# Feed-forward of the sample: first products by Strassen's scheme, their squares through DRAM, second products as a stage of their own

## The chip, the cores and the metric

One core of one Trainium2 chip runs the whole program. The metric is the device time in microseconds of one execution; for the kernel before it is 2505.32 us, the median of three runs (2496.89 to 2509.4). The engines are TensorE (PE in the rows, its weight loads PEld), VectorE (DVE), ScalarE (ACT), GpSimd (POOL) and SyncE (SP, which here only issues DMAs). POOL issues DMAs too, on a queue of its own.

## The reference, cut to what matters

One encoder layer is applied to two sequences: a prompt of 512 tokens and a sample of 1024, both 1024 wide, with the same weights. The change concerns the second half of the layer, for the sample:

```
u = _layer_norm(x) * (1.0 + sc2) + sh2
h = jnp.dot(jnp.square(jax.nn.relu(jnp.dot(u, w_ff1))), w_ff2)
x = _layer_norm_affine(ALPHA * x + (1.0 + g2) * h, ln_ff_g, ln_ff_b)
```

`w_ff1` is 1024 x 4096 and `w_ff2` 4096 x 1024, all in float32.

## The kernel before

Everything lies in tiles of 128 partitions. Tokens are worked on in chunks of 512: the prompt is one chunk, the sample two. A float32 operand is split into a rounded part and a remainder (`hi`, `lo`; `fp32r` in the rows), and a product of two such pairs is three matmuls into one PSUM bank (`mm3`, lines 112 to 114). ACT makes the rounded part and DVE the remainder; `wunit` (lines 88 to 94) does so for a weight block of 128 x 1024 that SP loads into one of three shared buffers (`wraw`), with a multiplication by a gain on POOL (line 90) where one is given.

The feed-forward is `ff`. It goes in eight groups of four blocks of 128 hidden channels. For each block, `wstat` multiplies the block's w1 with the 8 k-tiles of u, for every chunk: 24 matmuls of 512 columns a chunk. ACT takes the positive part (line 859), DVE squares (860), and the square is split into hh and hl (863, 864). When four blocks are there, the second products follow: per chunk 4 token tiles and 2 halves of the output, each 12 matmuls, added into the running output y by DVE (885). The last group treats the chunks one after the other, so w1 is read a third time for its four blocks; there x1 is added (845 to 847) and w2 carries the gain, and each finished token tile is normed (`ln_stats`, lines 128 to 143) and stored (`ff_store`, 913 to 922). The prompt's feed-forward comes first, woven with the norm of the sample's second chunk; then `ff_load` (lines 821 to 825) loads and splits the sample's u from DRAM, and the sample's feed-forward runs over two chunks at once.

The order on each engine is set by a planner, which takes the instructions as the program emits them and moves one forward where, by its own cost estimates, its inputs and its buffer are ready; each engine then keeps that order. `weave` sets the emission: it steps the generator with the least progress. Pools are stacks on the left and right side of SBUF; a pool opened over a closed one waits tile by tile for the old tiles' last use.

## Time and profile before

| | |
|---|---|
| median of three runs | 2505.32 us |
| profiled execution, own time | 2501.49 us |
| its span (first to last instruction) | 2499.7 us |
| PE busy | 2380.8 us (95%), 10992 matmuls |
| DVE busy | 1479.1 us (59%) |
| ACT busy | 973.2 us (39%) |
| POOL busy | 483.6 us (19%) |
| mean granted TensorE clock | 0.980 of full speed |
| chain that ended last | PE 68%, DVE 10%, issue 8%, DMA 6% |

The profile is one execution. A busy PE means that matmuls are in flight; they overlap, so the spacing of their starts says how fast they go, not their own length. An idle time stands with the instruction before which it lay and with what ended it.

### The profile page before, as it was taken

To read this page: it belongs to the slowest core of one execution; us is meant where nothing else is said; L and a number is where in the kernel's file an instruction comes from. 1 tells how busy PE (TensorE), PEld (TensorE's weight loads), DVE (VectorE), ACT (ScalarE), POOL (GpSimd) and SP (SyncE) were. 2 spreads that over 40 slices of the span, in tenths; PEclk is the share of its full clock that TensorE was granted. 3 is DMA by queue.
4 is the path that set the end of the run, shared out by engine and by line. 5 is a ranking of instruction groups with operands and counts; after the bars stand their busy time and mean duration, and the time that the engine had idled before them with its cause. 6 is when DMAs were issued, how large, how long until landed. Compare 5 with 4: busy or idle time off the path is not lost.

```text
span 2499.7 us, 29827 instructions
## 1 busy us (share of the span) xinstructions
PE 2380.8 (95%) x10992; PEld 1896.8 (76%) x10992; DVE 1479.1 (59%) x2511; ACT 973.2 (39%) x1589; POOL 483.6 (19%) x524
## 2 busy tenths in 40 slices
PE   5989999988999999999999999998999999999997
PEld 3867777756777777777777788886888888888876
DVE  6998686464677754675967844445733333333466
ACT  4434656434677754553434233232411211221122
POOL 4341242443000014432322000003100000000133
PEclk9999999988999999999999999999999999999999
DMA  6767634576212127655656435233511210211231
GB/s 250 253 220 229 213 129 158 145 208 206 64 55 74 51 73 203 175 190 189 212 194 230 147 101 160 69 118 122 163 42 34 68 51 20 66 57 36 68 110 60
DMA packets 124227, 325.85 MB, mean 130 GB/s; under 512 B 20240, under 2 KB 35632, under 8 KB 124080
## 3 DMA queue, kind: packets, MB, share of 16 engines
q1 hardware_dynamic: 105744, 266.21, 34.8%
q0 software_dynamic: 18048, 57.69, 6.6%
q8 instruction: 87, 1.43, 0.2%
q14 instruction: 60, 0.49, 0.1%
q10 hardware_dynamic: 288, 0.03, 0.0%
HBM read 261.99 MB, written 62.93 MB: 130 GB/s over the span
## 4 chain that ended last, share of the span: by engine, by line
PE 68%; DVE 10%; issue 8%; DMA 6%; POOL 3%; ACT 2%; SPq 0%; POOLq 0%; DVEq 0%; ACTq 0%
PE D L112 18%; PE D L114 18%; PE D L113 18%; PE S L534 3%; PE T L552 3%; PE A L680 2%; DVE wlo L94 2%; PE A L565 2%; PE A L566 1%; PE T L673 1%; ACT whi L93 1%; PE S L657 1%; DMA wraw<-in_wada 1%; DVE junk L248 1%; DMA og<-g 1%
## 5 line engine op out<-in xcount | busy, mean ns | idle before, releaser
L93 ACT ACTIVATE whi<-wraw 128x1024 fp32r<-128x1024 f32 x266 | 279.3, 1057 | 839.2 <-PE D L114 408.1
L114 PE MATMUL D<-uh,wlo 128*128 128x512 f32 x1344 | 533.5, 397 | 8.5 <-DVE wlo L94 8.5
L112 PE MATMUL D<-uh,whi 128*128 128x512 f32 x1344 | 536.1, 399 | 3.3 <-DVE stk L341 1.3
L113 PE MATMUL D<-ul,whi 128*128 128x512 f32 x1344 | 532.6, 396 | 0.0
L94 DVE TENSOR_TENSOR wlo<-wraw,whi 128x1024 fp32r<-128x1024 f32 x250 | 315.9, 1265 | 300.7 <-ACT whi L93 299.6
L112 PE MATMUL D<-whi,hh 128*128 128x512 f32 x768 | 304.8, 398 | 8.0 <-ACT hh L863 7.8
L114 PEld LDWEIGHTS D<-uh,wlo 128*128 128x128 f32 x1344 | 255.3, 190 | 66.2 <-DVE wlo L94 10.8
L114 PE MATMUL D<-whi,hl 128*128 128x512 f32 x768 | 303.8, 398 | 0.8 <-DVE hl L864 0.6
L113 PE MATMUL D<-wlo,hh 128*128 128x512 f32 x768 | 303.3, 397 | 0.0
L112 PEld LDWEIGHTS D<-uh,whi 128*128 128x128 f32 x1344 | 255.3, 190 | 58.6 <-issue 2.4
L113 PEld LDWEIGHTS D<-ul,whi 128*128 128x128 f32 x1344 | 255.6, 190 | 53.7 <-issue 0.9
L885 DVE TENSOR_TENSOR y<-y,D 128x512 f32<-128x512 f32 x168 | 115.2, 686 | 214.6 <-PE D L114 214.1
L112 PEld LDWEIGHTS D<-whi,hh 128*128 128x128 f32 x768 | 145.5, 190 | 45.2 <-ACT hh L863 11.9
L846 POOL TENSOR_TENSOR y<-y,g 128x1024 f32<-128x1024 f32 x12 | 28.8, 2401 | 753.7 <-DVE y L885 753.7
L114 PEld LDWEIGHTS D<-whi,hl 128*128 128x128 f32 x768 | 145.3, 190 | 37.2 <-DVE hl L864 3.6
L113 PEld LDWEIGHTS D<-wlo,hh 128*128 128x128 f32 x768 | 145.7, 190 | 33.4
L537 DVE TENSOR_REDUCE m<-S 128x1 f32<-128x1024 f32 (+1 forms) x96 | 99.7, 1041 | 44.5 <-PE S L534 44.3
L112 PE MATMUL D<-whi,uh 128*128 128x512 f32 (+1 forms) x288 | 107.1, 374 | 13.6 <-DVE stk L341 7.7
L556 DVE TENSOR_TENSOR pl<-T,ph 128x512 fp32r<-128x512 f32 x160 | 107.0, 684 | 14.6 <-ACT ph L555 13.7
L555 ACT ACTIVATE ph<-T 128x512 fp32r<-128x512 f32 x160 | 93.4, 596 | 52.1 <-PE T L552 50.4
L113 PE MATMUL D<-wlo,uh 128*128 128x512 f32 (+1 forms) x288 | 105.7, 367 | 3.1 <-DVE wlo L94 3.1
L114 PE MATMUL D<-whi,ul 128*128 128x512 f32 (+1 forms) x288 | 105.3, 366 | 0.0
(172 smaller groups left out, 3862.1 us busy)
## 6 DMA issues: line engine op xcount, KB each, us to landing
wraw<-in_w SPq DMA_DIRECT2D x132, 512.0 KB
wraw<-in_wst SPq DMA_DIRECT2D x56, 512.0 KB
wraw<-in_wada SPq DMA_DIRECT2D x32, 512.0 KB
g<-gst POOLq DMA_DIRECT2D x48, 256.0 KB, 3.2
og<-g SPq DMA_DIRECT2D x48, 256.0 KB
wraw<-in_wab SPq DMA_DIRECT2D x24, 512.0 KB
wraw<-in_wo SPq DMA_DIRECT2D x24, 512.0 KB
raw<-in_wada_k SPq DMA_DIRECT2D x16, 512.0 KB
```

The costliest lines, as they stand in the source:

```text
L93: nc.scalar.activation(hi, raw, AF.Copy)
L94: (engine or nc.vector).tensor_tensor(lo, raw, hi, op=ALU.subtract)
L112: mm(out, l[0], r[0], start=start, stop=False)
L113: mm(out, l[0], r[1], start=False, stop=False)
L114: mm(out, l[1], r[0], start=False, stop=stop)
L534: nc.tensor.matmul(S[:, k * CH:(k + 1) * CH], q, K[r][:, k * CH:(k + 1) * CH], start=r == 0, stop=r == 1)
L537: nc.vector.tensor_reduce(m, S[:, :T], axis=AX.X, op=ALU.max, negate=True)
L552: nc.tensor.transpose(tp[:, qt * P:(qt + 1) * P], Ps[qt][:, k * P:(k + 1) * P], self.ident)
L555: nc.scalar.activation(ph, tp, AF.Copy)
L556: nc.vector.tensor_tensor(pl, tp, ph, op=ALU.subtract)
L565: nc.tensor.matmul(acc, V[:, k, :], ph, start=k == 0, stop=False)
L885: nc.vector.tensor_tensor(y[:, hs], y[:, hs], ps, op=ALU.add)
```

## The change

Two blocks of hidden channels (a pair) and the two chunks of the sample make a 2 x 2 scheme, with the inner dimension of 1024 halved too. In place of the eight block products of 512 x 512 (per pair 8 x 4 x 3 matmuls), seven are computed from sums of weight halves and of u halves, and DVE sums them up out of PSUM (`ff1_pairs`). The sums of u are made on POOL while the prompt's feed-forward runs (`sums_first`); two of them, and u itself, go through DRAM and are loaded again (`sums_next`, `sums_last`). The sums of weights are made on POOL one pair ahead (`pair_weights`), whose w1 come by POOL's queue. The squares go to DRAM and not into SBUF. When all 16 pairs are done, `ff2_groups` runs the second products as a stage of their own, in the same eight groups of four blocks, each group's w2 and squares loaded one group ahead into two alternating places; the gain and x1 are added behind group 6, and the last group covers both chunks in one go. The prompt keeps `ff`, with fewer buffers, with its outputs stored by POOL's queue, and with its last tile's tail on POOL as for the other tiles.

```diff
-                        hh = pool.tile([P, CH], F32R, tag="hh", name="hh", bufs=8)
-                        hl = pool.tile([P, CH], F32R, tag="hl", name="hl", bufs=8)
+                        hh = pool.tile([P, CH], F32R, tag="hh", name="hh", bufs=6)
+                        hl = pool.tile([P, CH], F32R, tag="hl", name="hl", bufs=6)
...
-                    Y = [[ypool.tile([P, D], F32, tag="y", name="y", bufs=8) for _ in range(TT)] for _ in chs]
+                    Y = [[ypool.tile([P, D], F32, tag="y", name="y", bufs=4) for _ in range(TT)] for _ in chs]
...
-                    self.ff_store(cst(), *late, tail=cs[-1] == len(chs) - 1)
+                    self.ff_store(cst(), *late)
...
+    def split(self, pool, raw, tag, bufs, engine=None):
+        hi = pool.tile([P, CH], F32R, tag="uh" + tag, name="uh", bufs=bufs)
+        lo = pool.tile([P, CH], F32R, tag="ul" + tag, name="ul", bufs=bufs)
+        if engine:
+            engine.tensor_copy(hi, raw)
+        else:
+            self.nc.scalar.activation(hi, raw, AF.Copy)
+        (engine or self.nc.vector).tensor_tensor(lo, raw, hi, op=ALU.subtract)
+        return hi, lo
+
+    def fetch(self, pool, src, tag, bufs, engine=None):
...
+        self.nc.sync.dma_start(lo.bitcast(F32), src)
+        self.nc.scalar.activation(hi, lo.bitcast(F32), AF.Copy)
+        (engine or self.nc.vector).tensor_tensor(lo, lo.bitcast(F32), hi, op=ALU.subtract)
+        return hi, lo
...
+    def sums_first(self, pool, raws, B):
...
+        for i in range(4):
+            r1, r2 = [raws.tile([P, D], F32, tag="raw", name="raw", bufs=2) for _ in range(2)]
+            nc.gpsimd.dma_start(r1, s["u2"][i][:, :])
+            nc.gpsimd.dma_start(r2, s["u2"][4 + i][:, :])
+            yield (i + 0.5) / 4
+            B["11"].append(self.split(pool, r1[:, ab], "s", 12, nc.gpsimd))
+            B["21"].append(self.split(pool, r2[:, ab], "s", 12, nc.gpsimd))
+            sub = lambda o, x, y: nc.gpsimd.tensor_tensor(o, x, y, op=ALU.subtract)
+            sub(r1[:, ab], r1[:, b], r1[:, ab])
+            nc.gpsimd.dma_start(s["t1"][i], r1[:, ab])
+            sub(r1[:, b], r2[:, b], r1[:, b])
+            nc.gpsimd.dma_start(s["t3"][i], r1[:, b])
+            sub(r2[:, b], r2[:, b], r1[:, ab])
+            B["t2"].append(self.split(pool, r2[:, b], "s", 12, nc.gpsimd))
+            sub(r2[:, ab], r2[:, ab], r2[:, b])
+            nc.gpsimd.dma_start(s["t4"][i], r2[:, ab])
+            yield (i + 1.0) / 4
+
+    def sums_next(self, pool, B):
+        for k in ("t1", "t3"):
+            for i in range(4):
+                B[k].append(self.fetch(pool, self.scr[1][k][i], "p", 8))
+
+    def sums_last(self, pool, B):
+        s = self.scr[1]
+        for i in range(4):
+            B["t4"].append(self.fetch(pool, s["t4"][i], "v", 8))
+        for i in range(4):
+            B["22"].append(self.fetch(pool, s["u2"][4 + i][:, CH:], "v", 8))
+
+    def pair_weights(self, p, fw, A, raws=None):
...
+            if early:
+                hi = fw.tile([P, D], F32R, tag="whi1", name="whi", bufs=2)
+                lo = fw.tile([P, D], F32R, tag="wlo1", name="wlo", bufs=2)
+            else:
+                hi = self.W.tile([P, D], F32R, tag="whi", name="whi", bufs=4)
+                lo = self.W.tile([P, D], F32R, tag="wlo", name="wlo", bufs=4)
+            nc.scalar.activation(hi, raw, AF.Copy)
+            nc.vector.tensor_tensor(lo, raw, hi, op=ALU.subtract)
+            return (hi[:, ab], lo[:, ab]), (hi[:, b], lo[:, b])
...
+        if p:
+            r1, r2 = [self.wraw(a["w1"][2 * p + j], queue=nc.gpsimd) for j in range(2)]
...
+        A["11"], A["12"] = halves(r1, not p)
+        yield
+        S = fw.tile([P, D], F32R, tag="wlo1", name="ws", bufs=2).bitcast(F32)
+        nc.gpsimd.tensor_tensor(S[:, ab], r2[:, ab], r2[:, b], op=ALU.add)
+        nc.gpsimd.tensor_tensor(S[:, b], S[:, ab], r1[:, ab], op=ALU.subtract)
+        A["s1"], A["s2"] = halves(S)
+        yield
+        w = fw.tile([P, D], F32R, tag="whi1", name="w22", bufs=2)
+        nc.scalar.activation(w[:, ab], r2[:, b], AF.Copy)
+        nc.vector.tensor_tensor(w[:, b], r2[:, b], w[:, ab], op=ALU.subtract)
+        A["22"] = (w[:, ab], w[:, b])
+        yield
+        nc.gpsimd.tensor_tensor(r2[:, ab], r1[:, ab], r2[:, ab], op=ALU.subtract)
+        nc.gpsimd.tensor_tensor(r2[:, b], r1[:, b], S[:, b], op=ALU.subtract)
+        A["s3"], A["s4"] = halves(r2)
+
+    def ff1_pairs(self, A, B, fw, pool):
...
+        def prod(l, r):
+            ps = self.dps()
+            for k in range(4):
+                ks = slice(k * P, (k + 1) * P)
+                self.mm3(ps, (l[0][:, ks], l[1][:, ks]), r[k], k == 0, k == 3)
+            return ps
+
+        def store(h, f, c):
+            nc.sync.dma_start(s["h"][f][:, c * CH:(c + 1) * CH], h)
+
+        def hidden(x, ps, f, c):
+            h = pool.tile([P, CH], F32, tag="h", name="h", bufs=5)
+            nc.vector.tensor_tensor(h, x, ps, op=ALU.add)
+            nc.vector.scalar_tensor_tensor(h, h, 0.0, h, op0=ALU.max, op1=ALU.mult)
+            store(h, f, c)
+
+        def part(x, ps):
+            u = pool.tile([P, CH], F32, tag="part", name="part", bufs=4)
+            nc.vector.tensor_tensor(u, x, ps, op=ALU.add)
+            return u
+
+        for p in range(16):
+            f, nxt = 2 * p, {}
+            ahead = self.pair_weights(p + 1, fw, nxt) if p < 15 else iter(())
+            ps = prod(A["11"], B["11"])
+            p1 = pool.tile([P, CH], F32, tag="part", name="part", bufs=4)
+            nc.scalar.activation(p1, ps, AF.Copy)
+            next(ahead, None)
+            hidden(p1, prod(A["12"], B["21"]), f, 0)
+            next(ahead, None)
+            u2 = part(p1, prod(A["s2"], B["t2"]))
+            ps = prod(A["s1"], B["t1"])
+            u4 = part(u2, ps)
+            next(ahead, None)
+            u3 = part(u2, prod(A["s3"], B["t3"]))
+            hidden(u3, ps, f + 1, 1)
+            next(ahead, None)
+            hidden(u3, prod(A["22"], B["t4"]), f + 1, 0)
+            hidden(u4, prod(A["s4"], B["22"]), f, 1)
...
+    def ff2_groups(self, places, ypool, cst):
...
+        def load(gi):
+            hpool, tag, homes = places[gi % 2]
+            W2, H = [], []
+            for f in range(G):
+                n = gi * G + f
+                W2.append(self.wunit(a["w2"][n], gain=g2 if gi == ng - 1 else None, **homes[f]))
+                raw = self.wraw(s["h"][n][:, :])
+                H.append([self.split(hpool, raw[:, c * CH:(c + 1) * CH], tag, 8) for c in range(2)])
+            return W2, H
+
+        nxt = load(0)
+        for gi in range(ng):
+            last = gi == ng - 1
+            (W2, H), late = nxt, None
+            if not last:
+                nxt = load(gi + 1)
+            for c in range(2):
+                for t in range(TT):
+                    y = Y[c][t]
+                    for hf in range(2):
+                        hs = slice(hf * CH, (hf + 1) * CH)
+                        ps = self.dps()
+                        for f in range(G):
+                            hh, hl = H[f][c]
+                            self.mm3(ps, (hh[:, t * P:(t + 1) * P], hl[:, t * P:(t + 1) * P]),
+                                     (W2[f][0][:, hs], W2[f][1][:, hs]), f == 0, f == G - 1)
+                        if gi == 0:
+                            nc.vector.tensor_copy(y[:, hs], ps)
+                        else:
+                            nc.vector.tensor_tensor(y[:, hs], y[:, hs], ps, op=ALU.add)
+                    if gi == ng - 2:
+                        t0 = c * CH
+                        x1 = self.wraw(s["x1"][t0 + t * P:t0 + (t + 1) * P, :])
+                        nc.gpsimd.tensor_tensor(y, y, g2, op=ALU.mult)
+                        nc.vector.scalar_tensor_tensor(y, x1, ALPHA, y, op0=ALU.mult, op1=ALU.add)
+                    if last:
+                        now = ((1, c * CH), t, y, *self.ln_stats(cst, [y], "f"))
+                        if late:
+                            self.ff_store(cst, *late)
+                        late = now
+            if last:
+                self.ff_store(cst, *late, tail=True)
...
-            nc.sync.dma_start(self.y[seq][t0 + t * P:t0 + (t + 1) * P, hs], y[:, hs])
+            (nc.sync if seq else nc.gpsimd).dma_start(self.y[seq][t0 + t * P:t0 + (t + 1) * P, hs], y[:, hs])
...
+                **{f"t{n}": [t(f"t{n}{i}_", [P, CH]) for i in range(4)] for n in (1, 3, 4)}, h=[t(f"h{i}_", [P, T]) for i in range(32)] if q else []))
...
-        w1 = [a["w1"][f] for f in range(32)]
-        ws = self.stream(w1 + w1 + w1[-4:], pool=wp, tag="1", bufs=2, ahead=1)
+        ws = self.stream([a["w1"][f] for f in range(32)], pool=wp, tag="1", bufs=2, ahead=1)
...
+            for x in self.sums_first(late["u"], late["raw"], B):
+                yield LN + 0.5 * x
...
-        US = [self.ff_load(scs[0], late["u"], "s"), self.ff_load(scs[1], upF, "p")]
-        self.weave(self.ff(scs, US, ws, hp, yp, consts))
-        for x in (y_st, h_st, late["ust"], late["st"], w_st, uF_st, psD_st):
+        A = {}
+        for _ in self.pair_weights(0, wp, A, late["raw"]):
+            pass
+        self.sums_next(upF, B)
+        late["rst"].close()
+        y_st.close()
+        h_st.close()
+        fv, fv_st = self.pool("fv", side="right")
+        fa, fa_st = self.pool("fa", side="right")
+        self.sums_last(fv, B)
+        self.weave(self.ff1_pairs(A, B, wp, fa))
+        late["ust"].close()
+        fa_st.close()
+        fv_st.close()
+        fh2, fh2_st = self.pool("fh2")
+        yp, y_st = self.pool("fy2", side="right")
+        own, fw, wts = dict(pool=fh2, tag="2", bufs=2), dict(pool=wp, tag="1", bufs=2), {}
+        self.ff2_groups([(fh2, "t", [own, own, fw, fw]), (upF, "p", [wts] * 4)], yp, late["pool"])
...
```

## Rows read from the trace of the kernel before

**Rows 1.** The page: engines (busy, share, instructions), and GB/s in 40 slices.

```profile
PE 2380.8 (95%) x10992; PEld 1896.8 (76%) x10992; DVE 1479.1 (59%) x2511; ACT 973.2 (39%) x1589; POOL 483.6 (19%) x524
...
GB/s 250 253 220 229 213 129 158 145 208 206 64 55 74 51 73 203 175 190 189 212 194 230 147 101 160 69 118 122 163 42 34 68 51 20 66 57 36 68 110 60
```

**Rows 2.** Busy time by stretches: length, each engine (x instructions), clock, DMA, GB/s.

```profile
core 0: us, PE busy (x) PEld busy (x) DVE busy (x) ACT busy (x) POOL busy (x), PEclk, DMA share, GB/s
...
1650.00:1700.00 50.00, 50.00 (x218) 40.63 (x217) 21.62 (x27) 11.67 (x15) 2.39 (x1) 1.00 0.24 75
1700.00:1767.00 67.00, 58.75 (x241) 46.67 (x241) 45.75 (x70) 24.44 (x35) 21.88 (x12) 0.95 0.49 149
1767.00:2406.00 639.00, 639.00 (x2762) 519.20 (x2761) 246.78 (x318) 132.15 (x182) 33.68 (x17) 1.00 0.20 61
2406.00:2471.00 65.00, 60.33 (x242) 46.81 (x241) 42.54 (x77) 19.53 (x27) 16.21 (x13) 0.95 0.22 73
```

**Rows 3.** Groups by form, 1767 to 2488 us: busy, mean ns, idle before, releaser.

```profile
L114 PE MATMUL D<-uh,wlo 128*128 128x512 f32 x512 | 202.2, 395 | 3.4 <-DVE wlo L94 3.4
L112 PE MATMUL D<-whi,hh 128*128 128x512 f32 x512 | 202.2, 395 | 0.3 <-ACT hh L863 0.3
...
L94 DVE TENSOR_TENSOR wlo<-wraw,whi 128x1024 fp32r<-128x1024 f32 x67 | 85.6, 1279 | 130.9 <-ACT whi L93 130.8
...
L93 ACT ACTIVATE whi<-wraw 128x1024 fp32r<-128x1024 f32 x67 | 70.1, 1058 | 404.2 <-PE D L114 235.1 <-DMA wraw<-in_w 100.1 <-PE D L113 52.7
L864 DVE TENSOR_TENSOR hl<-h,hh 128x512 fp32r<-128x512 f32 x64 | 44.2, 691 | 37.1 <-ACT hh L863 37.1
...
L921 POOL TENSOR_TENSOR y<-y,lnfb 128x512 f32<-128x512 f32 x16 | 23.3, 1463 | 22.2 <-DVE y L920 20.8 <-DVE rs_t L133 1.4
...
L847 DVE SCALAR_TENSOR_TENSOR y<-wraw,y 128x1024 f32<-128x1024 f32 x8 | 12.0, 1497 | 20.3 <-POOL y L846 20.3
```

**Rows 4.** Timeline of PE, 2406 to 2413 us: start, length, instruction.

```profile
2406.26 0.40 PE L113 MATMUL D<-ul,whi 128*128 128x512 f32 x1
2408.80 0.67 PE L114 MATMUL D<-uh,wlo 128*128 128x512 f32 x1 [2.15 <-DVE wlo L94]
...
2412.55 0.40 PE L114 MATMUL D<-uh,wlo 128*128 128x512 f32 x1
```

**Rows 5.** Timeline, DVE beside POOL, at 1715 and at 2429 us.

```profile
1715.05 2.39 POOL L90 TENSOR_TENSOR wraw<-wraw,g 128x1024 f32<-128x1024 f32 x1
1715.13 3.40 DVE L847 SCALAR_TENSOR_TENSOR y<-wraw,y 128x1024 f32<-128x1024 f32 x1 [2.52 <-POOL y L846]
...
2429.48 0.68 DVE L885 TENSOR_TENSOR y<-y,D 128x512 f32<-128x512 f32 x1
2429.64 1.29 POOL L921 TENSOR_TENSOR y<-y,lnfb 128x512 f32<-128x512 f32 x1 [3.61 <-DVE y L920]
...
2430.08 1.41 DVE L920 TENSOR_TENSOR y<-y,lnfg 128x512 f32<-128x512 f32 x1
```

**Rows 6.** Timeline at the prompt's end, 1718 to 1784 us: SP, PE and DVE.

```profile
1718.55 12.70 SPq L88 DMA_DIRECT2D wraw<-in_w  x5
...
1737.57 21.98 SPq L821 DMA_DIRECT2D wraw<-u  x14
...
1744.78 0.80 PE L112 MATMUL D<-whi,hh 128*128 128x512 f32 x1 [3.70 <-ACT hh L863]
...
1747.50 0.68 DVE L825 TENSOR_TENSOR ul<-wraw,uh 128x512 fp32r<-128x512 f32 x1
...
1781.53 2.43 SPq L922 DMA_DIRECT2D out_y_prompt<-y  x2
```

**Rows 7.** Timeline of POOL in the last four tiles' norm.

```profile
2473.09 0.55 POOL L129 TENSOR_TENSOR rs<-rs_v,mhalf 128x1 f32<-128x1 f32 x1 [18.97 <-DVE rs_v L128]
...
2485.89 0.55 POOL L129 TENSOR_TENSOR rs<-rs_v,mhalf 128x1 f32<-128x1 f32 x1
```

**Rows 8.** DMA issues by POOL: one in the timeline, and size and time to landing.

```profile
1360.01 0.54 POOL L811 DMA_DIRECT2D u<-uf  x1 [1.55 <-ACT uf L173]
...
u<-uf POOLq DMA_DIRECT2D x24, 256.0 KB, 4.2
```

More of the change, by code (lines that the diff above doesn't have):

```diff
@@ new lines, in fetch, with wraw @@
+    def fetch(self, pool, src, tag, bufs, engine=None):
+        hi = pool.tile([P, CH], F32R, tag="uh" + tag, name="uh", bufs=bufs)
+        lo = pool.tile([P, CH], F32R, tag="ul" + tag, name="ul", bufs=bufs)
+        self.nc.sync.dma_start(lo.bitcast(F32), src)
+        self.nc.scalar.activation(hi, lo.bitcast(F32), AF.Copy)
+        (engine or self.nc.vector).tensor_tensor(lo, lo.bitcast(F32), hi, op=ALU.subtract)
+        return hi, lo
+    def wraw(self, src, n=D, queue=None):
+        raw = self.W.tile([P, n], F32, tag="wraw", name="wraw", bufs=3)
+        (queue or self.nc.sync).dma_start(raw, src)
+        return raw
@@ new lines, in sums_first @@
+    def sums_first(self, pool, raws, B):
+        nc, s = self.nc, self.scr[1]
+        ab, b = slice(0, CH), slice(CH, 2 * CH)
+        for i in range(4):
[15 more added lines that the diff above has]
+            yield (i + 1.0) / 4
@@ new lines, in sums_next, with halves @@
+    def sums_next(self, pool, B):
[9 more added lines that the diff above has]
+    def pair_weights(self, p, fw, A, raws=None):
+        nc, a = self.nc, self.a
+        ab, b = slice(0, CH), slice(CH, 2 * CH)
+        def halves(raw, early=False):
+            if early:
[10 more added lines that the diff above has]
+        else:
+            r1, r2 = [raws.tile([P, D], F32, tag="raw", name="raw", bufs=2) for _ in range(2)]
+            nc.gpsimd.dma_start(r1, a["w1"][0])
+            nc.gpsimd.dma_start(r2, a["w1"][1])
+        A["11"], A["12"] = halves(r1, not p)
[13 more added lines that the diff above has]
+        A["s3"], A["s4"] = halves(r2)
+        yield
@@ new lines, in ff1_pairs @@
+    def ff1_pairs(self, A, B, fw, pool):
+        nc, s = self.nc, self.scr[1]
+        def prod(l, r):
[33 more added lines that the diff above has]
+            hidden(u4, prod(A["s4"], B["22"]), f, 1)
+            A = nxt
+            yield (p + 1.0) / 16
@@ new lines, in ff2_groups @@
+    def ff2_groups(self, places, ypool, cst):
+        nc, a, s = self.nc, self.a, self.scr[1]
+        G = 4
+        ng = FF // P // G
+        g2 = self.ff_consts(cst, 1)
+        Y = [[ypool.tile([P, D], F32, tag="y", name="y", bufs=8) for _ in range(TT)] for _ in range(2)]
+        def load(gi):
[25 more added lines that the diff above has]
+                            nc.vector.tensor_copy(y[:, hs], ps)
+                        else:
+                            nc.vector.tensor_tensor(y[:, hs], y[:, hs], ps, op=ALU.add)
[11 more added lines that the diff above has]
+                self.ff_store(cst, *late, tail=True)
@@ L934, in scratch @@
                 g=[t(f"g{i}_", [P, T]) for i in range(16)], oa=t("oa_", [512, T]), ob=t("ob_", [512, T]),
-                x1=t("x1_", [T, D]), u2=[t(f"u2{i}_", [P, T]) for i in range(KT)]))
+                x1=t("x1_", [T, D]), u2=[t(f"u2{i}_", [P, T]) for i in range(KT)],
+                **{f"t{n}": [t(f"t{n}{i}_", [P, CH]) for i in range(4)] for n in (1, 3, 4)}, h=[t(f"h{i}_", [P, T]) for i in range(32)] if q else []))
     def run(self):
@@ L1082, in consts @@
             return late["pool"]
-        w1 = [a["w1"][f] for f in range(32)]
-        ws = self.stream(w1 + w1 + w1[-4:], pool=wp, tag="1", bufs=2, ahead=1)
+        ws = self.stream([a["w1"][f] for f in range(32)], pool=wp, tag="1", bufs=2, ahead=1)
         ffp = self.ff([pc], [UF], ws, hp, yp, consts)
+        B = {k: [] for k in ("11", "21", "22", "t1", "t2", "t3", "t4")}
         def last_norm():
@@ L1094, in last_norm @@
             late["u"], late["ust"] = self.pool("fu")
+            late["raw"], late["rst"] = self.pool("fr")
+            for x in self.sums_first(late["u"], late["raw"], B):
+                yield LN + 0.5 * x
         self.weave(last_norm(), ffp)
-        US = [self.ff_load(scs[0], late["u"], "s"), self.ff_load(scs[1], upF, "p")]
-        self.weave(self.ff(scs, US, ws, hp, yp, consts))
-        for x in (y_st, h_st, late["ust"], late["st"], w_st, uF_st, psD_st):
+        A = {}
[16 more added lines that the diff above has]
+        self.ff2_groups([(fh2, "t", [own, own, fw, fw]), (upF, "p", [wts] * 4)], yp, late["pool"])
+        for x in (y_st, fh2_st, late["st"], w_st, uF_st, psD_st):
             x.close()
```

2 lines of the change are left out of this document (1 added, 1 removed).

## Prediction

> **What bounds the kernel now.** First PE's share of the span, 95% [rows 1]; 2501.5 us is the profiled execution's own time, 1.8 us more than its span. Then the feed-forward by stretches. The sample's part runs from 1767 to 2488 us. From 1767 to 2406, PE is busy without a break at granted clock 1.00 and starts 2762 products: 639.00 / 2762 = 0.2314 us each. From 2406 to 2471, 242 products take 65.00 us where 242 x 0.2314 = 56.0 would do: 9.0 us are lost. At the end of the prompt's part (1700 to 1767), 241 products take 67.00 us: 11.2 us lost. Between 1650 and 1700 PE loses nothing while DVE works 21.62 of 50.00 us [rows 2]. By forms: the six product groups have 512 entries each (two 513), so 1536 first products (operands u and w1) and 1536 second ones (h and w2). PE waits 3.4 us for a w1 remainder there and hardly otherwise [rows 3]. So the stage is bound by the number of products, and other engines count only where PE runs dry. What that costs: products start at 2406.26 and next at 2408.80, and the nine intervals from there to 2412.55 take 3.75 us, seven of them near 0.43, which is the lower of the clock's two levels (1.2 for 2.4 GHz), after PE had stood still; (2.54 - 0.23) + (3.75 - 9 x 0.2314) = 4.0 us for one dry spot [rows 4].
>
> **The products.** Before: 32 blocks x 2 chunks x 8 k x 3 = 1536 first products. After: 16 pairs x 7 x 4 x 3 = 1344. Second products stay 1536. Removed: 192 x 0.2314 = **-44.4 us**, all of it on the path. The forms are the same (128x128 by 128x512), so the interval is kept.
>
> **The last group's halves.** Before, the last group ran per chunk, with w1 read again for the second chunk, w2 multiplied by the gain on POOL (L90, 2.39 us each [rows 5]), and the chain product, relu, square, hh, hl, second product laid bare. After, no first products stand there and the last group's w2 are made a group earlier. The 9.0 us go: **-9.0** (ends -9 and 0).
>
> **The pairs (taken at 0).** PE needs 7 x 4 x 3 = 84 products, 19.4 us a pair. DVE per pair, by mean durations: three remainders of 1024 columns at 1.28 (L94), one of 512 at 0.69 (L864), seven sums out of PSUM at 0.68 (L885 in [rows 5]), four squares at 0.75 (half of L847, the same form at 1024 columns): 3.8 + 0.7 + 4.8 + 3.0 = 12.3 us. ACT: 3 x 1.06 and two of half that size, 4.2. POOL: four sums of 512, 1.46 each (L921) [rows 3]: 5.9, and two issues at 0.54 [rows 8]. Weights are prepared a pair ahead, so the cover is 19.4 - 12.3 = 7.1 us of DVE per pair and the eight PSUM banks, 8 x 12 x 0.2314 = 22.2 us of products. POOL eats into it: L847 on DVE, two SBUF operands, took 3.40 us where it began beside POOL's L90 (which starts 0.08 us before it and takes 2.39), against a mean of 1.50 in the sample's stretch [rows 3]; L920 took 1.41 beside L921, while L885, with one operand in PSUM, took 0.68 beside the same L921 [rows 5]. The Trainium skill, page "SBUF — State Buffer", section "Who interferes with whom", says that a DVE instruction with two SBUF inputs and a GpSimd instruction that reads SBUF shut each other out for a whole instruction; the trace agrees (3.40 us, of which 2.31 beside L90). By the DVE rows alone a pair costs DVE 12.3 us, by that rule at worst 18.2; both lie under 19.4, which is why the rule leaves the sum but feeds a rival. From the rows: with all of POOL's 5.9 us laid on DVE, 18.2 of 19.4. Bounds: 0 to +75 (the rival below); no gain, since PE stood without a break already. The squares' stores are 64 of 256 KB on SP's queue, behind which no load stands until the second stage; 16.8 MB out and in again is nothing beside the 61 GB/s that this stretch moved when the busiest slices moved 250 [rows 1, 2]. Cost 0.
>
> **Prompt to sample.** Pair 0 needs its first weights, B11 and B21, and these are made during the prompt's last group. Its weights s1/s2 need buffers that the prompt's last w2 hold until PE ends there (1767): ACT 1.06, DVE 1.28, perhaps behind 2 us of norm work, and products 1 and 2 cover 2 x 12 x 0.2314 = 5.6 us. The order is one that already mixes such loads with the prompt's end: a u remainder (L825) runs at 1747.50, twenty microseconds before the prompt's PE end [rows 6]. t4 and the half 22 are eight loads of 256 KB; the 14 before took 21.98 us, 1.57 each [rows 6], so the last lands some 13 to 15 us after 1767, with 22 wanted by product 7 at 6 x 2.78 = 16.7. The buffers of the squares lie over the prompt's y: the last two stores issue from 1781.53 on, in 2.43 us [rows 6], 15 to 17 us after PE's end, and now leave by POOL's queue (landing 4.2 us [rows 8]); the first square waits for them, and behind it on DVE the sums of products 3 to 7, and PE only where its ninth product has no bank, at 22.2 us. Just hidden. **+2** (0 to +11, the loss of [rows 2] at the prompt's end).
>
> **First to second stage.** The first group's buffers lie over B11, B21 and t2, free after product 3 of the last pair; PE then has 4 x 2.78 = 11.1 us. Eight loads of 512 KB through three buffers: three are there already, five at 2.5 us (12.70 for five [rows 6]) end about 13 us on, with split 15 to 16; PE wants the fourth block at 11.1 + 9 x 0.2314 = 13.2. About 2.5 us dry and 1.7 at the lower level [rows 4]: **+4** (0 to +11).
>
> **Second stage.** Per group PE has 192 x 0.2314 = 44.4 us; DVE 16 x 0.69 + 4 x 1.28 + 8 x 0.69 = 21.7. Group 6 adds eight y times gain (POOL, the form of L90, 2.39) and L847 (1.50, and DVE idle 20.3 / 8 = 2.5 for each [rows 3]): 21.7 + 32 = 54, about 9 us over 44.4, held by the banks (22.2). In the last group the norm of a tile takes 6.40 us by POOL's rs (2473.09 to 2485.89 is two tiles [rows 7]) while PE needs 24 x 0.2314 = 5.56; before, four tiles in a row lagged so. Now eight run in a row: 4 x 0.84 = 3.4 more, and part of group 6's lag. **+8** (+3 to +16).
>
> **Prompt's part.** The sums on POOL: 40 instructions of 512 columns, 40 x 1.46 = 58 us, between 0.35 and 0.85 of the prompt's 355 us (1536 products), where DVE has half its time free [rows 2]; each can hold up one DVE instruction. In the other direction PE's 3.70 us gap at 1744.78, left by the sample's loads on ACT [rows 6], may be filled. **+2** (-5 to +8). hh/hl 8 to 6 and y 8 to 4: 0; one chunk needs four, and the next group's products come behind this group's on PE. The third reading of four w1 goes, off the path.
>
> **Sum.** -44.4 - 9.0 + 0 + 2 + 4 + 8 + 2 = -37.4. From 2501.5: 2464; the median shown, 2505.3, lies 3.8 higher and would give 2468. I say **2465**.
>
> **Rivals.** *Slower: DVE runs the pairs.* Each remainder L94 waited 130.9 / 67 = 1.95 us for ACT [rows 3]; if the three of a pair keep that, 18.2 + 3 x 1.95 = 24.1 us, 4.7 over PE's 19.4, x 16 = 75 us: 2540. Or PE runs dry once a pair, 16 x 4.0 = 64: 2529. It decides from (37 + 12.5) / 16 = 3.1 us a pair. For: the lock of [rows 5]. Against: those waits fell where DVE had 61% idle (246.78 of 639 busy [rows 2]), and weights come a pair ahead. 0.06. *No gain: the pairs run at 22.2 us*, the old 96 products' time: 16 x 2.8 = 44 back: 2509. 0.10. *Small gain: every seam at its upper end*, 11 + 11 + 16 + 4: -53.4 + 42 = -11, and cases halfway: 2476 to 2492. For: pools now lie on one another at three seams. 0.18. *Larger gain: seams hidden, tail +3:* -50: 2451. 0.14. The rest, 0.52, is the forecast's own band, 2455 to 2476.
>
> **Numbers.** A measurement of this kernel can tell 0.5%, 12.5 us: faster means under 2492.8. Faster 0.52 + 0.14 + 0.18 = 0.84, same 0.10, slower 0.06. Range 2442 to 2496: the interval of 1650 to 1700 is 50.00 / 218 = 0.2294, 6 us less over 2880 products, and the small-gain case fits in whole.
>
> **What would show it.** First products of the sample: 1344 at 0.23 us; PE unbroken in all but the first pair; DVE near 12 us of each 19.4. A dry PE of 2 to 5 us before the first second product; last evacuation 5 us or more after its product. Wrong: PE waiting for DVE sums or a w remainder within pairs, or an interval above 0.24 at clock 1.00.

## The result and the profile after

The changed kernel takes 2472.13 us (median of four runs, 2466.86 to 2478.57) against 2505.15 beside it: ratio 0.987, 95% interval 0.984 to 0.991. Timed once more with five rounds it took 2479.32 against 2498.65: 0.991 (0.988 to 0.994). The profiled execution took 2466.86 us, its span 2465.1, at granted clock 0.98.

(A product is one matmul below; a block product is one of the seven of a pair, twelve matmuls.) First the engines on the page of the changed kernel, which answers [rows 1]:

```profile
PE 2328.5 (94%) x10800; PEld 1854.7 (75%) x10800; DVE 1584.7 (64%) x2649; ACT 968.6 (39%) x1570; POOL 668.2 (27%) x690
```

PE has exactly 192 matmuls fewer, and DVE 105.6 and POOL 184.6 us more. Where each stage stands is read from the windows of the changed kernel (columns as in [rows 2]): the prompt's middle and end, the seam to the sample, the pairs, the second products, the end.

```profile
1534.00:1604.00 70.00, 64.05 (x269) 50.83 (x268) 37.91 (x37) 21.47 (x29) 47.90 (x48) 0.98 0.62 202
...
1694.00:1768.00 74.00, 65.25 (x263) 51.27 (x262) 48.74 (x69) 21.92 (x31) 34.08 (x24) 0.91 0.37 125
1768.00:1801.00 33.00, 22.02 (x81) 16.16 (x81) 29.34 (x40) 11.79 (x19) 24.23 (x21) 0.79 0.42 143
1801.00:2097.00 296.00, 295.93 (x1280) 239.97 (x1279) 182.33 (x236) 69.61 (x81) 96.03 (x78) 1.00 0.34 113
2097.00:2448.00 351.00, 349.64 (x1525) 285.70 (x1523) 185.55 (x286) 71.57 (x99) 47.07 (x28) 1.00 0.33 106
2448.00:2465.00 17.00, 0.29 (x2) 0.00 (x0) 11.58 (x28) 2.40 (x4) 7.21 (x6) 0.60 0.25 93
```

The pairs run without a break, 296.00 / 1280 = 0.231 us a product, DVE at 62%; so do the second products but for 1.4 us. PE loses time in three stretches: at the seam, 11.0 of 33 us idle at clock 0.79; at the prompt's end (1694 to 1768), 8.75 us, about as before (8.25 [rows 2]); and in the prompt's middle (1534 to 1604), 5.95 us, where POOL now works 47.90 us and 202 GB/s move. The middle of the kernel before lost 0.09:

```profile
1540.00:1610.00 70.00, 69.91 (x305) 56.70 (x304) 34.42 (x41) 24.84 (x33) 1.65 (x4) 1.00 0.44 143
```

Groups by form of the changed kernel, 1768 to 2465 us (columns as in [rows 3]):

```profile
L112 PE MATMUL D<-whi,uh 128*128 128x512 f32 x512 | 201.0, 393 | 1.4 <-ACT uh L904 1.4
...
L112 PE MATMUL D<-uh,whi 128*128 128x512 f32 x384 | 150.8, 393 | 0.0
...
L969 DVE TENSOR_TENSOR wlo<-wraw,whi 128x1024 fp32r<-128x1024 f32 x30 | 39.6, 1321 | 3.6 <-ACT whi L968 3.6
...
L113 PE MATMUL D<-ul,w 128*128 128x512 f32 x64 | 26.6, 416 | 4.3 <-DVE ul L914 4.2
L112 PE MATMUL D<-uh,w 128*128 128x512 f32 x64 | 26.3, 412 | 6.7 <-ACT uh L913 6.7
```

384 + 64 = 448 first products per form, 1344 in all as counted. All waiting of first products stands in the two rows of 64, the products with `w` (block 22 of w1): they wait for t4's rounded part (L913) and then for its remainder (L914). The w1 remainders L969 wait 3.6 us in all for ACT.

**Stages side by side.** From start times of single products and the span, of one profiled execution each, in us. Prompt: from the first second product (`whi,hh`) to the sample's first product. Sample: from there to the start of the last product. End: from there to the end of the span.

| kernel | prompt starts | prompt | sample | end | own time |
|---|---|---|---|---|---|
| before | 1415.6 | 351.5 | 720.3 | 12.3 | 2501.49 |
| after | 1409.1 | 359.2 | 679.6 | 17.2 | 2466.86 |
| after, again | 1421.0 | 361.2 | 678.9 | 17.4 | 2480.22 |
| eighth product | 1415.4 | 358.1 | 723.6 | 16.8 | 2515.82 |
| t4 and 22 rounded by DVE | 1421.7 | 360.4 | 681.8 | 17.7 | 2483.41 |
| sums on DVE | 1419.3 | 367.0 | 679.0 | 17.6 | 2484.81 |
| before, one last group | 1417.2 | 348.7 | 710.8 | 15.3 | 2493.83 |
| DVE load | 1416.4 | 359.5 | 680.3 | 17.8 | 2475.76 |
| pairs turned | 1412.8 | 362.7 | 669.0 | 17.4 | 2463.59 |
| end half on DVE | 1410.4 | 358.5 | 679.0 | 20.0 | 2469.76 |
| no pair 1 weights | 1417.1 | 359.9 | 677.4 | 17.1 | 2473.33 |
| few sums | 1426.8 | 360.2 | 678.8 | 17.3 | 2484.99 |
| few loads | 1422.4 | 353.5 | 680.0 | 17.3 | 2475.01 |
| pairs turned, again | 1414.5 | 359.7 | 670.3 | 17.6 | 2463.85 |

The start column is a part of the program that no experiment touches; it ranges over 17.7 us, and the changed kernel itself stands at 1409.1 and 1421.0. The other columns repeat within 3 us for the same kernel, so the experiments are read by them. From before to after: prompt +7.7, sample -40.7, end +4.9: the feed-forward gained 28.1 us, and the remaining 6.5 of the two profiles' difference is the first column's spread. (Some expectations below carry earlier readings of these columns, up to 0.5 us off.)

**The seam.** The timeline of the changed kernel, PE, ACT, DVE, POOL and SP together, ordered by start:

```profile
1769.83 1.85 SPq L912 DMA_DIRECT2D ul<-u  x4
...
1772.10 0.68 DVE L885 TENSOR_TENSOR y<-y,D 128x512 f32<-128x512 f32 x1
...
1777.54 1.74 POOL L1117 TENSOR_TENSOR y<-y,lnfb 128x512 f32<-128x512 f32 x1
...
1778.11 2.25 DVE L969 TENSOR_TENSOR wlo<-wraw,whi 128x1024 fp32r<-128x1024 f32 x1
...
1780.16 0.63 POOL L129 TENSOR_TENSOR rs<-rs_v,mhalf 128x1 f32<-128x1 f32 x1
...
1781.92 0.39 PE L114 MATMUL D<-uh,wlo 128*128 128x512 f32 x1
...
1785.27 0.16 DVE L1109 SCALAR_TENSOR_TENSOR nm<-mv,rs 128x1 f32<-128x1 f32 x1
...
1785.46 1.52 ACT L1115 ACTIVATE y<-y,nm,rs 128x512 f32<-128x512 f32 x2 [7.99 <-DVE nm L1109]
...
1788.31 3.22 ACT L913 ACTIVATE uh<-ul 128x512 fp32r<-128x512 f32 x6
...
1788.98 0.79 PE L112 MATMUL D<-uh,w 128*128 128x512 f32 x1 [6.67 <-ACT uh L913]
...
1792.23 1.73 DVE L914 TENSOR_TENSOR ul<-ul,uh 128x512 fp32r<-128x512 f32 x1
...
1794.01 0.79 PE L113 MATMUL D<-ul,w 128*128 128x512 f32 x1 [4.24 <-DVE ul L914]
```

PE finishes five block products and stops at 1781.92 with t4 wanted. SP had issued the last load by 1771.7, and from 1778 to 1780 nothing moves on any queue, so the loads have landed (windows of the same kernel):

```profile
1778.00:1780.00 2.00, 2.00 (x11) 1.65 (x10) 2.00 (x3) 0.00 (x0) 1.70 (x2) 1.00 0.00 0
```

But on ACT the six splits (L913) stand behind the norm of the prompt's last token tile (L1115), for which ACT sat idle 7.99 us; that norm goes from DVE's last addition (1772.10) by POOL's rs (1780.16, behind POOL's L1117 and a store's issue) to nm at 1785.27, and between its steps DVE works at the norm of the tile before and at remainders of pair 1's weights, the one at 1778.11 drawn out to 2.25 us beside POOL. So ACT, the engine that t4 waits for, stands idle with t4 in its buffers. Then the first remainder L914 begins only at 1792.23, behind four sums and squares on DVE. Two stops: (7.06 - 0.23) + (5.03 - 0.23) = 11.6 us. Behind the second, the ten intervals from 1794.01 to 1799.25 take 5.24 us where 2.3 would do: the granted clock is 0.50 there, its lower level, after PE had stood still, and the next remainders are waited for shortly. From the sample's first product on, 120 products take 42.46 us, 14.7 more than at 0.2314 each; that is the price of the seam.

Of the end, the timeline of the changed kernel (PE, POOL, DVE):

```profile
2412.96 0.56 POOL L129 TENSOR_TENSOR rs<-rs_v,mhalf 128x1 f32<-128x1 f32 x1 [4.42 <-DVE rs_v L128]
...
2447.90 0.39 PE L114 MATMUL D<-whi,ul 128*128 128x512 f32 x1
...
2451.34 0.55 POOL L129 TENSOR_TENSOR rs<-rs_v,mhalf 128x1 f32<-128x1 f32 x1
...
2455.28 0.68 DVE L1078 TENSOR_TENSOR y<-y,D 128x512 f32<-128x512 f32 x1
```

From rs to rs a tile takes (2451.34 - 2412.96) / 6 = 6.40 us, as in [rows 7], and now for eight tiles in a row. The last addition begins 7.38 us after the last product begins; in the kernel before that was 2.45:

```profile
2487.39 0.39 PE L114 MATMUL D<-whi,hl 128*128 128x512 f32 x1
...
2489.84 0.68 DVE L885 TENSOR_TENSOR y<-y,D 128x512 f32<-128x512 f32 x1
```

### The profile page after: what moved, and what is told of

Same layout as the page of the kernel before. It is cut to its first block, busy times and chain, and to the rows that moved or that the text cites. A ratio compares the mean times of both kernels' runs of the same rounds, so it can differ in the third digit from the quotient of the medians.

```text
span 2465.1 us, 30146 instructions
## 1 busy us (share of the span) xinstructions
PE 2328.5 (94%) x10800; PEld 1854.7 (75%) x10800; DVE 1584.7 (64%) x2649; ACT 968.6 (39%) x1570; POOL 668.2 (27%) x690
## 4 chain that ended last, share of the span: by engine, by line
PE 61%; DVE 12%; issue 9%; DMA 8%; POOL 4%; ACT 3%; SPq 1%; POOLq 0%; ACTq 0%; DVEq 0%
PE D L112 16%; PE D L113 16%; PE D L114 16%; PE S L534 3%; PE T L552 3%; DVE wlo L94 2%; PE A L680 2%; PE A L565 2%; PE A L566 1%; ACT whi L93 1%; DMA wraw<-in_w 1%; PE T L673 1%; PE S L657 1%; DVE junk L248 1%; POOL y L1117 1%
## 5 line engine op out<-in xcount | busy, mean ns | idle before, releaser
L112 PE MATMUL D<-uh,whi 128*128 128x512 f32 x1216 | 483.1, 397 | 4.2 <-DVE stk L341 1.7
L112 PE MATMUL D<-whi,uh 128*128 128x512 f32 (+1 forms) x800 | 308.1, 386 | 9.6 <-ACT gst L497 3.7
L113 PE MATMUL D<-wlo,uh 128*128 128x512 f32 (+1 forms) x800 | 305.2, 382 | 2.8 <-DVE wlo L94 2.8
L114 PE MATMUL D<-whi,ul 128*128 128x512 f32 (+1 forms) x800 | 304.7, 381 | 0.1
L112 PEld LDWEIGHTS D<-whi,uh 128*128 128x128 f32 x800 | 152.1, 190 | 41.9 <-ACT gst L497 4.7
L113 PEld LDWEIGHTS D<-wlo,uh 128*128 128x128 f32 x800 | 151.8, 190 | 32.1 <-DVE wlo L94 3.3
L114 PEld LDWEIGHTS D<-whi,ul 128*128 128x128 f32 x800 | 151.7, 190 | 30.6 <-DVE ul L905 0.5
L537 DVE TENSOR_REDUCE m<-S 128x1 f32<-128x1024 f32 (+1 forms) x96 | 99.7, 1041 | 44.7 <-PE S L534 44.4
L112 PE MATMUL D<-whi,hh 128*128 128x512 f32 x256 | 103.6, 407 | 14.1 <-ACT hh L863 14.1
L114 PE MATMUL D<-whi,hl 128*128 128x512 f32 x256 | 102.3, 404 | 1.3 <-DVE hl L864 1.3
L540 ACT ACTIVATE P<-S,m 128x1024 f32<-128x1024 f32 (+1 forms) x96 | 93.3, 972 | 24.6 <-DVE m L537 23.5
```

The costliest lines, as they stand in the source:

```text
L112: mm(out, l[0], r[0], start=start, stop=False)
L113: mm(out, l[0], r[1], start=False, stop=False)
L114: mm(out, l[1], r[0], start=False, stop=stop)
L537: nc.vector.tensor_reduce(m, S[:, :T], axis=AX.X, op=ALU.max, negate=True)
L540: nc.scalar.activation(p, S[:, :T], AF.Exp, bias=m, scale=1.0, accum_out=z)
```

## The experiments

**The products by themselves.** An eighth block product in each pair, computed and not used:

```
             hidden(u3, prod(A["22"], B["t4"]), f + 1, 0)
+            prod(A["22"], B["t4"])
             hidden(u4, prod(A["s4"], B["22"]), f, 1)
```

> The changed kernel with an eighth product put back into each pair (A22 with t4 once more, into a bank that nobody reads). Theory (the gain is the products that go): the pair grows from 84 to 96 matmuls, 16 x 12 x 0.2314 = 44.4 us more in the pairs' stage, 2465 to about 2510 us of span, and PE still without a break there. Rival (the pairs run at another engine's pace, DVE's or the stores'): PE has room in a pair, and the stage grows by less than 20 us.

The sample's part took 723.6 us, 44.0 more for 192 products: 0.229 each, with the pairs still unbroken. The products are worth what they were priced at.

**The last group's halves.** The kernel before, its last group with both chunks in one go:

```
-for cs in ([[c] for c in range(len(chs))] if last else [range(len(chs))]):
+for cs in [range(len(chs))]:
-self.stream(w1 + w1 + w1[-4:], ...
+self.stream(w1 + w1, ...
```

> The kernel before with one part of the change alone: the last group of the sample takes both chunks in one go, with no third reading of four w1 blocks. Theory: of the 9.4 us that PE loses from 2406 us on, most stay, since the first products and the chain relu, square, split still stand ahead of the last group's second products there, so at most 5 us are gained; and the norms of eight tiles in a row, 6.40 us each against 5.56 us of products, put 3 to 5 us behind PE's end (11.9 us before). Together -2 to +4 us. Rival, as predicted: all 9 us go and the end costs 8: -1 us, with no dry PE in the last group.

Windows of this kernel, over its sample part:

```profile
1766.00:2476.00 710.00, 710.00 (x3070) 577.03 (x3069) 291.21 (x417) 151.04 (x207) 54.10 (x35) 1.00 0.19 59
```

Not one dry spot is left: 3070 products at 0.2313. The sample's part fell by 9.5 us, and the end grew by 3.0, since eight tiles in a row are normed here too. The theory set down before the run, that most of the loss stays, was wrong; the rival, which is the prediction's term, held.

**Room on DVE in the pairs.** Two more passes of `h = max(h, h)` over each square, 6.0 us of DVE a pair as measured:

```
+            for _ in range(2):
+                nc.vector.tensor_tensor(h, h, h, op=ALU.max)
```

> The changed kernel with two more DVE instructions (h = max(h, h), 512 columns, two SBUF operands) behind each square: eight a pair, 8 x 0.69 = 5.5 us. In the changed kernel DVE is busy 182.3 of 296 us in the pairs, 11.95 us of each 19.4, and this time already holds its waits behind POOL. Theory (DVE has 7 us to spare in a pair): PE keeps standing without a break in the pairs and the stage grows by less than 5 us. Rival (POOL's 6 us come on top of DVE's time, and the waits for ACT too): 12 + 5.5 + 6 = 23.5 us a pair against 19.4, and the stage grows by 40 to 65 us.

Windows of this kernel, 296 us of the pairs:

```profile
1812.00:2108.00 296.00, 296.00 (x1282) 240.30 (x1281) 273.98 (x359) 69.40 (x80) 97.81 (x78) 1.00 0.34 112
```

DVE at 93% and PE unbroken; the sample's part grew by 0.7 us. Ahead of this window, in pair 0, PE stopped a third time, for 1.70 us at 1804.95, for a remainder of t4 (L914). The slower rival, DVE runs the pairs, is refuted with room to spare.

**Whose queue holds the seam?** First, t4 and the half 22 rounded by DVE and not by ACT:

```
-self.nc.scalar.activation(hi, lo.bitcast(F32), AF.Copy)
+self.nc.vector.tensor_copy(hi, lo.bitcast(F32))    # for t4 and 22
```

> The changed kernel with the rounded parts of t4 and of the half 22 (eight copies of 512 columns) made by DVE and not by ACT. Theory (in pair 0 PE waits for these copies because they stand on ACT behind the norm of the prompt's last tile, which started at 1785.5 us): the two waits of PE of 7.06 and 5.03 us at the seam shrink to 3 us or less together, the stretch from the sample's first product to full speed is 8 to 11 us shorter. Rival (the loads of t4 and 22 land late, because their buffers lie over the prompt's): the waits stay, at 10 us or more, and the DVE copies wait for a DMA.

Timeline of this kernel at the seam, DVE and PE:

```profile
1799.08 0.16 DVE L1112 SCALAR_TENSOR_TENSOR nm<-mv,rs 128x1 f32<-128x1 f32 x1
...
1801.77 1.95 DVE L972 TENSOR_TENSOR wlo<-wraw,whi 128x1024 fp32r<-128x1024 f32 x1 [0.25 <-ACT whi L971]
...
1806.04 2.86 DVE L914 CAST uh<-ul 128x512 fp32r<-128x512 f32 x2
...
1807.55 0.80 PE L112 MATMUL D<-uh,w 128*128 128x512 f32 x1 [11.45 <-DVE uh L914]
```

The theory that ACT's queue alone is to blame fell: the first stop grew from 7.06 to 11.84 us, the second fell from 5.03 to 3.08, and the sample's part grew by 2.2. On DVE the rounding stands behind the same norm, a weight remainder and the pairs' additions. Late data is not the cause either: SP issued the last of these loads by 1785.9, and DVE took up the first 20 us later, busy with other work.

Then pair 1 given pair 0's weights, so that their preparation leaves the seam:

```
-ahead = self.pair_weights(p + 1, fw, nxt) if p < 15 else iter(())
+ahead = self.pair_weights(p + 1, fw, nxt) if 0 < p < 15 else iter(())
-A = nxt
+A = nxt if p else A
```

> The changed kernel in which pair 1 takes the weights of pair 0, so that the weights of pair 1 are neither loaded nor summed nor split: at the seam 6.1 us of DVE go and four sums of POOL with them. Theory (the seam's wait is DVE's queue with POOL's lock): PE's two waits, 7.06 and 5.03 us, fall by 8 us or more together. Rival (ACT's order behind the norm of the prompt's last tile alone): the copies of t4 still start where that norm ends, and the waits fall by 4 us at most.

Timeline of this kernel, ACT and PE:

```profile
1792.63 1.52 ACT L1115 ACTIVATE y<-y,nm,rs 128x512 f32<-128x512 f32 x2 [6.91 <-DVE nm L1109]
...
1794.53 3.73 ACT L913 ACTIVATE uh<-ul 128x512 fp32r<-128x512 f32 x7
1795.20 0.80 PE L112 MATMUL D<-uh,w 128*128 128x512 f32 x1 [4.16 <-ACT uh L913]
```

The two stops fell from 12.09 to 8.14 us, just within the 4 us that the rival allowed, and the sample's part by 2.2. The splits still follow the last norm at once, as the rival said; but the planner pulled pair 2's weights into the place that was freed (its sums run on POOL at 1781.03), so this run does not say what the seam would be without weights.

Last, the block products that want t4 and 22 moved behind the first five of pair 1 (with two `part` buffers more and one `h` fewer, and the preparation of pair 2's weights begun behind pair 0's last block products; cut here):

```
+late.append((A, u3, u4, f))
+while p and late:                 # nothing in pair 0, both pairs' in pair 1
+    A_, u3, u4, f = late.pop(0)
-    hidden(u3, prod(A["22"], B["t4"]), f + 1, 0)
-    hidden(u4, prod(A["s4"], B["22"]), f, 1)
+    hidden(u3, prod(A_["22"], B["t4"]), f + 1, 0)
+    hidden(u4, prod(A_["s4"], B["22"]), f, 1)
```

> The changed kernel with the order of the first two pairs turned: pair 0 products 1 to 5, pair 1 products 1 to 5, then the last two of each, so that t4 and the half 22 are wanted 5 x 2.78 = 13.9 us later; six buffers for parts, four for squares, weights of pair 2 begun behind pair 0's last products. Theory (at the seam DVE has a queue of some 12 us, in which the splits of t4 and 22 come last, while their data have lain ready since about 1777 us): the two waits of 7.06 and 5.03 us fall to 3 us or less, and the sample's products from first to last take 8 to 12 us less than 679.85. Rival (whatever comes last on DVE is waited for, now the sums of pair 1 or weights): PE stands as long, somewhere in the first two pairs, and 679.85 changes by less than 3.

Timeline of this kernel, ACT, DVE and PE:

```profile
1792.69 1.52 ACT L1126 ACTIVATE y<-y,nm,rs 128x512 f32<-128x512 f32 x2 [8.02 <-DVE nm L1120]
...
1795.55 1.14 ACT L913 ACTIVATE uh<-ul 128x512 fp32r<-128x512 f32 x2
...
1801.63 0.69 DVE L1011 TENSOR_TENSOR h<-part,D 128x512 f32<-128x512 f32 x1 [4.46 <-DMA out_y_prompt<-y]
1802.38 0.50 PE L112 MATMUL D<-uh,whi 128*128 128x512 f32 x1 [1.78 <-DVE h L1011]
```

The norm comes as late as before and so do the splits, but PE has ten block products to go before it wants them: the sample's part fell by 10.6 us to 669.0. Only now does the wait show that the prediction had in mind for this place: a first sum in h's buffer (L1011) waits 4.46 us for the store of the prompt's y, and PE 1.8 us for its bank.

Not tested: the splits of t4 put ahead of that norm on ACT, which stood idle for 7.99 us.

**The prompt's part.** Its 8 us were put to three runs. First, the sums and splits on DVE and ACT and not on POOL:

```
-B["11"].append(self.split(pool, r1[:, ab], "s", 12, nc.gpsimd))    # 21, t2 likewise
+B["11"].append(self.split(pool, r1[:, ab], "s", 12))
-sub = lambda o, x, y: nc.gpsimd.tensor_tensor(o, x, y, op=ALU.subtract)
+sub = lambda o, x, y: nc.vector.tensor_tensor(o, x, y, op=ALU.subtract)
```

> The changed kernel with the u sums and splits during the prompt's feed-forward on DVE and ACT in place of POOL (12 splits and 16 differences). Theory (POOL's instructions shut DVE out there, so hh, hl and the w remainders come late): the prompt's feed-forward from its first second product to the sample's first product falls from 359 us towards the 351.5 of the kernel before, by 5 to 8 us, although DVE gets 19 us more work. Rival (it is DVE's order, which waits for the sums' loads and for the prompt's products in turn): the prompt's part stays at 359 us or grows by up to 10.

Timeline of this kernel, ACT and PE:

```profile
1557.29 0.63 ACT L904 ACTIVATE uh<-raw 128x512 fp32r<-128x512 f32 x1 [8.88 <-DMA raw<-u]
1557.83 1.04 ACT L93 ACTIVATE whi<-wraw 128x1024 fp32r<-128x1024 f32 x1
1558.92 0.80 PE L112 MATMUL D<-uh,whi 128*128 128x512 f32 x1 [6.90 <-ACT whi L93]
```

The prompt's part went up by another 7.8 us to 367.0, on the rival's side: a split on ACT waits 8.88 us for its u to arrive, and the prompt's weight stands behind it. POOL is the better place because this wait holds up nobody there.

Second, 34 of the 40 sums and splits left out, the transfers kept:

```
+if i == 0:
     B["11"].append(self.split(...)); B["21"]..., B["t2"]...
+else:
+    for k in ("11", "21", "t2"): B[k].append(B[k][0])
-sub(r1[:, ab], r1[:, b], r1[:, ab])      # and the three others
```

> 34 of the 40 sums and splits that POOL makes in the prompt's part are left out; the loads and stores around them stay, the sample's first products then read wrong operands, and the number of products stays. Theory: the prompt's part went from 351.0 to 359.0 us because these instructions shut DVE out, so it falls back to 351 to 354 us; the sample's part stays at 679 to 682 us. Rival: the 8 us come from the order and the loads of the changed prompt part, not from POOL's work: then the prompt's part stays at 357 to 360 us.

Third, the loads and stores of three of the four rounds left out too:

```
+if i == 0:
     nc.gpsimd.dma_start(r1, s["u2"][i][:, :])    # and r2, and the stores
```

> As the kernel with few sums, and the loads and stores of three of the four rounds are left out too (each round's loads are 1.0 MB and its stores 0.75 MB); the sample's first products read wrong operands, and the number of products stays. Theory: the transfers of the sums hold up the prompt's w1 loads, so the prompt's middle (some 70 us around the sums), which lost 5.9 us of PE in the changed kernel and still 4.1 with few sums, loses under 1 us, and the prompt's part falls to 353 to 357 us; the loss at the prompt's end (8.8 to 11.5 us) stays. Rival: the transfers don't matter and the planner's order alone costs it: the middle still loses 3 us or more, and the prompt's part stays at 358 to 362 us.

Windows of the prompt's middle, with few sums:

```profile
1552.00:1622.00 70.00, 65.91 (x276) 52.08 (x275) 33.27 (x39) 22.69 (x30) 18.03 (x28) 0.98 0.72 248
```

and of its middle and end, with few loads:

```profile
1546.00:1616.00 70.00, 67.01 (x292) 54.02 (x291) 35.32 (x40) 23.21 (x31) 15.49 (x18) 1.00 0.54 173
...
1706.00:1776.00 70.00, 60.07 (x250) 47.62 (x250) 50.94 (x68) 22.42 (x32) 31.38 (x23) 0.95 0.38 132
```

With few sums POOL's work in the middle fell from 47.90 to 18.03 us, PE's loss there from 5.95 to 4.09, and the prompt's part stayed at 360.2: the theory that POOL shuts DVE out fell. With few loads it was 353.5, 6.7 less, within 2.0 of the kernel before, as the theory of the transfers said. (Each is one execution, and this part differed by up to 3.0 us between two executions of one kernel.) Its finer point missed: the middle still loses 3.0 us, all at one stop. The end loses 9.9 us there, against 8.25 before [rows 2].

**The end.** The upper half's last addition of each tile on DVE:

```
-(nc.vector if tail else nc.gpsimd).tensor_tensor(y[:, hs], y[:, hs], self.lnfb[:, hs], op=ALU.add)
+(nc.vector if tail or (seq and hf) else nc.gpsimd).tensor_tensor(...)
```

> The changed kernel with the last addition of the norm (lnfb) of the sample's upper half columns on DVE in place of POOL. Theory (the last group's tile takes 6.40 us because DVE waits 1.2 us for POOL's rs, which stands behind two additions of 1.46): DVE gets 0.69 us more and loses the wait of 1.2, a tile takes 5.6 to 5.9 us, and the last tile's sum comes 3 to 5 us sooner after the last product; 16.8 us from the last product's end to the end of the span become 12 to 14. Rival (DVE is the limit there): 6.40 stays or becomes 7, and the end comes later by up to 5 us.

Timeline of this kernel, POOL's rs:

```profile
2441.46 0.55 POOL L129 TENSOR_TENSOR rs<-rs_v,mhalf 128x1 f32<-128x1 f32 x1 [1.48 <-DVE rs_v L128]
...
2447.88 0.55 POOL L129 TENSOR_TENSOR rs<-rs_v,mhalf 128x1 f32<-128x1 f32 x1 [1.49 <-DVE rs_v L128]
```

A tile still takes 6.42 us though POOL now waits, and the end grew by 2.8: moving the addition only trades POOL's time for DVE's, as the rival had it.

**Timed against each other.** The kernel with the pairs turned and the changed kernel, five rounds each:

> The version with the order of the first two pairs turned, timed in five rounds. Theory: the 10.9 us that its sample part lost less than the changed kernel's stay in the median: about 10 us below the changed kernel's median beside it (some 2461 against 2472), 0.982 of the kernel before. Rival: the prompt's part and the part ahead take the gain back (its prompt part took 362.7 us against 359.0): then the two medians lie within 4 us.

> The changed kernel as it is, timed in five rounds on the same chip as the version with the order turned: about 2470 us, 0.987 of the kernel before, by every theory. Its profile shows how far the part ahead of the feed-forward moves from one execution to the next: theory, that the 6.5 us which it took less in the first profile are spread, so that the first hh product of the prompt starts between 1409 and 1422 us and its sample part takes 679 to 681 us again; rival, that the changed kernel always reaches it at 1409 us.

Pairs turned: 2463.85 us (2455.78 to 2467.94), 0.985 of before (0.983 to 0.988). Changed kernel: 2479.32 (2471.30 to 2481.17), 0.991 (0.988 to 0.994). The version with the pairs turned beats both, the changed kernel by 15.5 us of median. In the two profiles, 16.4 us apart, the sample's part makes 678.9 - 670.3 = 8.6 of it, the prompt's 1.5, and 6.5 lie in the first column of the table. Whether that last part is chance is not shown: in these rounds the longest run of the one is shorter than the shortest of the other. The changed kernel came to the feed-forward at 1421.0 this time, 12 us later than in its first profile.

## Why the prediction was right, and where it was not

The time came 7 us above the forecast, within its range. By stages the feed-forward gained 28.1 us where the sum said 37.4, and 6.5 of what was missing came back by the start column, which the prediction did not speak of: to that extent the closeness is luck. Against the kernel before beside it the median gained 33.0 us in the first timing and 19.3 in the second, whose 2479.32 lies in the band that the prediction gave to a small gain. Term by term:

- **Products, -44.4:** right (44.0 for the same count added back).
- **Last group's halves, -9.0:** right (9.5 in the kernel before alone).
- **Pairs, 0:** right. DVE took 182.33 / 296.00 x 19.4 = 11.95 us a pair (12.3 said); the squares' trip through DRAM cost nothing that PE saw. A remainder (L969) took 2.25 us beside POOL's L1117 against a mean of 1.32. The Trainium skill, page "SBUF — State Buffer", section "Who interferes with whom", says that a DVE instruction with two SBUF inputs contends with a GpSimd instruction that reads SBUF; this row agrees. Even with DVE at 93% of the pairs' time PE did not wait there.
- **Prompt to sample, +2:** mis-sized, and beyond its bounds (0 to +11): 11.6 us of stops and some 3 more behind them, 14.7. The step that failed is the one for t4 and the half 22. It priced the landing of their loads ("the last lands some 13 to 15 us after 1767") and put the place of their splits in the queues of ACT and DVE at nothing; norm work stood in the term once, as 2 us ahead of other weights. The loads were in time (by 1778, 10 us after the sample's first product), but the norm's chain from the last addition to ACT's L1115 took 1785.46 - 1772.10 = 13.4 us. Some 5 of these are its own steps by their durations; the rest are waits, because its small steps alternate between POOL and DVE and queued there behind other work, on DVE the tile before and pair 1's weights. ACT split t4 only after it, and DVE made the remainders after that. Shown by turning the pairs (-10.6), and by DVE being no better a place than ACT. The lower clock behind a stop, which the term for the second stage has with 1.7 us, was left out here. The wait that was priced (a square for the prompt's store) was real but came later.
- **First to second stage, +4:** two product starts lie 1.75 us apart there, 1.75 - 0.23 = 1.5, below the value taken.
- **End, +8:** 4.9. Eight tiles in a row cost 3.0 in the kernel before with one last group (3.4 said). The lag of group 6 never stopped PE; the other 1.9 us fit what was left of it: the additions of the last group's second tile begin 1.9 and 1.7 us after their last products, against 1.0 and 0.7 with one last group.
- **Prompt, +2:** mis-sized, 7.7, near its upper end. The failed step is the price itself: it counted POOL's 40 instructions and left their transfers out. Those are four rounds of 1.0 MB in and 0.75 MB out, most of them within the 70 us of the middle, which moved 143 GB/s before and 202 now. Leaving out instructions did not shorten the part, leaving out transfers gave 6.7 us back. The gap at the prompt's end was not filled: t1 and t3 now come through ACT where u came before, and ACT waits 1.26, 1.14 and 1.37 us for three of these loads (1739 to 1743) ahead of the hh that PE wants.

Together -44.4 - 9.5 + 14.7 + 1.5 + 4.9 + 7.7 = -25.1, against -28.1 measured; most of the rest is the sample's other products, which came at 0.2304 and not 0.2314 (2.8 us). Still open: by which transfer each stop of the prompt's middle was caused (the weight loads' time in the queues was not taken apart), and why the part ahead of the feed-forward wanders by 18 us. Of the signs that the prediction named, the unbroken pairs, DVE's 12 us of each 19.4 and the late last addition (7.38 us) came; the dry PE ahead of the second products was 1.5 us and not 2 to 5.

## What to carry to other kernels

Price the seams of a new stage by queue order: for each operand the new stage wants first, list what stands ahead of it on the engine that makes it, and follow a chain of small steps between two busy engines step by step; most of it can be queue waits (here some 8 of 13.4 us) and not its own durations. An engine that stands idle while an operand behind its next instruction is ready is a sign of such an order. Where such an operand was late here, an order that put independent products ahead of it was worth more than moving its making to another engine. When work is moved to an idle engine, price its transfers apart from its instructions, and read experiments by stages when an untouched part varies by as much as the effect.
